# Shift and scale of the first layer: VectorE sums five of eight row blocks, and one unread product is left out

## The chip, the cores and the metric

The kernel runs on one core of one Trainium2 chip, as one program. The metric is the device time of one execution in microseconds (us).

## What is computed

Two blocks of two layers each, on 512 positions of width 1024, in 32-bit floats. The part that matters here is the start of the first layer: from a vector `c` six vectors of width 1024 are made, and the first two, shift and scale, enter the normalized input ahead of the layer's first product.

```python
c_act = jax.nn.silu(c)
mod = c_act @ w_ada + b_ada                     # 1024 -> 6 * 1024
shift1, scale1, gate1, shift2, scale2, gate2 = jnp.split(mod, 6, axis=-1)
h = modulate(rms_norm(x, norm1_g), shift1, scale1)     # h * (1 + scale1) + shift1
... = jnp.split(h @ w_in, split_points, axis=-1)
```

Everything behind that (retention, gated linear attention, forgetting attention, the feed-forward parts, and the second block with its pooling and windowed attention) is the same in both kernels.

## The kernel before, in words

All activations lie transposed: `x[k]` holds 128 of the 1024 features (k = 0 to 7) by 512 positions. Weights stream through the kernel as 486 chunks `w` of eight 128x128 tiles. A product in full precision is made from three matmuls in a faster 32-bit format (`mm3`, lines 219 to 221): every operand is split in a high and a low part, `wh` and `wl` for weights, `h[k][:, 0]` and `h[k][:, 1]` for activations, and the products high by high, high by low and low by high are added in PSUM. For each chunk ScalarE casts `wh` (line 184) and VectorE subtracts for `wl` (line 193); `prep_to(c)` issues both for all chunks up to c.

The schedule is manual: each engine executes its instructions in the order in which the Python code issues them, and waits at each for what that instruction needs.

The opening is `start_group` (line 1094). It computes the first seven output tiles of `h @ w_in` (`nj` = 7), and makes shift, scale and `h` block by block as it goes:

- `ada_dma(k)` loads, for block k, the 256 columns of `w_ada` (128 of shift and 128 of scale) in two tiles of 128x(4x256): the row blocks kk = 0 to 3 and 4 to 7 of the 1024 rows.
- `ada_pe(k)` (line 1128) multiplies the eight row blocks with `cpad[:, kk]`, a 128x32 tile whose column 0 is `c_act` and whose other columns are zero. Each such matmul fills 32 columns of TensorE's array, and four lie side by side (`tile_position=(0, c)`); row blocks 4 to 7 are a second round on the same four places. The result is one row of 256 in each of four groups of 32 PSUM partitions. ScalarE copies it to `row` (line 1134).
- `ada_ab(k)` (line 1138) adds the four groups and turns the row into two columns, with two matmuls against a column of ones (line 1141); VectorE adds the bias (line 1143) and forms (1 + scale) times the norm's gain (line 1144). The two columns of `AB` are what this text calls AB of block k.
- `norm_s(k)`: VectorE makes `nt` = x times AB's scale times the reciprocal norm (line 324), ScalarE adds the shift and rounds to the high half of `h[k]` (line 329), VectorE subtracts for the low half (line 336).

Ahead of the loop stand the sum of squares, its sum over the partitions (`colsum`, line 296), the reciprocal root on GpSimd (line 301), and `bcast` (line 306), which spreads the reciprocal norm over the partitions. In between, `busy(k)` (line 1158) issues a product of `ident` and `x[k]` into a PSUM buffer that nobody reads.

The loop over k is the place of the change. One step multiplies block k with its seven tiles. After the tiles j = 0, 1 and 4 the work for later blocks is woven in (`early`):

```python
if i == 0:      norm_s(k + 1, pB)
elif i == 1:    ada_pe(k + 2); prep_to(...)
elif i == 2:    ada_ab(k + 2)
```

In step 0 the order is a different one: the seven tiles are passed three times, and `ada_pe(1)`, `ada_pe(2)` and their `ada_ab` stand between the passes.

PSUM holds five buffers `mm` and three `sd`. Seven of the eight carry the seven sums of the loop; the last `sd` serves `ada_pe` and `ada_ab` of one block after the other.

Of the kernel before, what the change touches and what calls it, by code (L numbers as in the profile page):

```python
# [10 lines left out]
F32 = mybir.dt.float32  # L11
F32R = mybir.dt.float32r
AF = mybir.ActivationFunctionType
ALU = mybir.AluOpType
# [93 lines left out]
def emit(tc, A, log, stop=None, dump=None):  # L108
    nc = tc.nc
    ctx = ExitStack()  # L110
    sb = ctx.enter_context(tc.tile_pool(name="sb", bufs=1))
# [4 lines left out]
    def nm(p):  # L116
        uid[0] += 1
        return f"{p}_{uid[0]}"

    def g4(p, dt=F32, shape=(128, 1024)):  # L120
        return sb.tile(list(shape), dt, tag="g4", bufs=NG, name=nm(p))

    def t2(p, dt=F32):
        return sb.tile([128, 512], dt, tag="t2", bufs=NT, name=nm(p))

    def c16(p, dt=F32):
        return sb.tile([128, 16], dt, tag="c16", bufs=20, name=nm(p))

    def mmb():
        return pp.tile([128, 512], F32, tag="mm", bufs=5, name=nm("mm"))  # L130

    def sdb():
        return pp.tile([128, 512], F32, tag="sd", bufs=3, name=nm("sd"))

    V, ACT, PL, PE = nc.vector, nc.scalar, nc.gpsimd, nc.tensor
# [24 lines left out]
    def pc(key, l=None, i=0, n=1):  # L160
        o = _PO[key if l is None else (key, l)] + i
        return par[:, o:o + n]
# [9 lines left out]
    def w_dma(c):  # L172
        while st["dma"] <= min(c, NCH - 1):
            t = g4("w")
            nc.sync.dma_start(t, wall[st["dma"]])
            stage[st["dma"]] = t
            st["dma"] += 1

    def w_hi(c):
        while st["hi"] <= min(c, NCH - 1):  # L180
            i = st["hi"]
            w_dma(i)
            his[i] = g4("wh", F32R)
            ACT.copy(his[i], stage[i])  # L184
            st["hi"] += 1

    def prep_to(c, eng=None):
        while st["prep"] <= min(c, NCH - 1):
            i = st["prep"]
            w_dma(i + 1 + LD)  # L190
            w_hi(i + st["ha"])
            l = g4("wl", F32R)
            (eng or V).tensor_tensor(l, stage.pop(i), his[i].bitcast(F32), op=ALU.subtract)  # L193
            prepped[i] = (his.pop(i), l)
            st["prep"] += 1
# [96 lines left out]
    def colsum(out, sq, c0, n):  # L292

        p = sdb()
        for i in range(n):
            PE.transpose(p[:, i * 128:(i + 1) * 128], sq[:, c0 + i * 128:c0 + (i + 1) * 128], ident)  # L296
        V.tensor_reduce(out, p[:, 0:n * 128].rearrange("p (a b) -> p a b", a=n), axis=AX.X, op=ALU.add)

    def rstd_of(r, n, dim):
        V.tensor_scalar(r, r, 1.0 / dim, EPS, op0=ALU.mult, op1=ALU.add)  # L300
        PL.tensor_tensor(r, r, mhalf[:, 0:n], op=ALU.pow)

    def bcast(ps, r, n):

        for i in range(n):
            PE.transpose(ps[:, i * 128:(i + 1) * 128], r[:, i:i + 1].to_broadcast([128, 128]), ident)
# [11 lines left out]
    def new_h():  # L318
        for k in range(8):
            h[k] = sb.tile([128, 2, 512], F32R, tag="h", bufs=8, name=nm("h"))  # L320
# [216 lines left out]
    cact = sb.tile([128, 8], F32, name="cact")  # L537
# [556 lines left out]
    def start_group(cons):  # L1094
        specs, evacs, view = cons
        nj = len(evacs)
        st["la"] = st["ha"] = 0
        cpad = sb.tile([128, 8, 32], F32, name="cpad")
        PL.memset(cpad, 0.0)
        ACT.activation(cact, pc("c", None, 0, 8), AF.Silu)  # L1100
        V.tensor_copy(cpad[:, :, 0], cact)
        at = {}

        def ada_dma(k):
            at[k] = []
            for j in range(2):
                t = g4("ada", shape=(128, 4, 256))
                nc.sync.dma_start(t, A["wada"][2 * k + j].rearrange("p (a b) -> p a b", a=4))
                at[k].append(t)

        for k in range(8):
            nc.sync.dma_start(x[k], A["xT"][k * 128:(k + 1) * 128])
        ada_dma(0)
        w_dma(0)
        ada_dma(1)
        w_dma(1)
        ada_dma(2)
        w_dma(2)
        ada_dma(3)
        ada_dma(4)  # L1120
        AB = c16("AB")
        bpair = c16("bp")
        V.tensor_copy(bpair.rearrange("p (k j) -> p j k", j=2), pc("bada", 0, 0, 16).rearrange("p (j k) -> p j k", j=2))
        Ac, Bc = (lambda k: AB[:, 2 * k + 1:2 * k + 2]), (lambda k: AB[:, 2 * k:2 * k + 1])
        pa, ra = {}, {}

        def ada_pe(k):

            pa[k] = p = sdb()
            for kk in range(8):  # L1130
                c = 32 * (kk % 4)
                PE.matmul(p[c:c + 32, 0:256], cpad[:, kk], at[k][kk // 4][:, kk % 4], start=kk < 4, stop=kk >= 4, tile_position=(0, c))
            ra[k] = t2("row")[:, 0:256]
            ACT.copy(ra[k], p[:, 0:256])
            del at[k]

        def ada_ab(k):

            p, row = pa.pop(k), ra.pop(k)
            for i in range(2):  # L1140
                PE.matmul(p[:, 256 + i:257 + i], row[:, i * 128:(i + 1) * 128], one, start=True, stop=True)
            ab = AB[:, 2 * k:2 * k + 2]
            V.tensor_tensor(ab, p[:, 256:258], bpair[:, 2 * k:2 * k + 2], op=ALU.add)
            V.tensor_scalar(ab[:, 1:2], ab[:, 1:2], 1.0, pc("n1", 0, k), op0=ALU.add, op1=ALU.mult)

        acc = sb.tile([128, 512], F32, tag="acc", bufs=1, name=nm("acc"))
        for k in range(8):
            if k == 0:
                ACT.activation(acc, x[k], AF.Square)
            else:  # L1150
                q = t2("sq")
                ACT.activation(q, x[k], AF.Square)
                V.tensor_tensor(acc, acc, q, op=ALU.add)
        spare = mmb()

        def busy(k):

            PE.matmul(spare, ident, x[k], start=True, stop=True)

        for k in range(5):  # L1160
            busy(k)
        r = c16("rs")
        colsum(r[:, 0:4], acc, 0, 4)
        rstd_of(r[:, 0:4], 4, D)
        ada_pe(0)
        ada_ab(0)
        busy(5)
        pb = sdb()
        bcast(pb, r, 4)
        busy(6)  # L1170
        new_h()
        w_hi(0)

        def norm_s(k, pB):
            t = norm_t(k, 0, 512, pB, Ac)
            norm_h(k, 0, 512, t, Bc)
            norm_l(k, 0, 512, t, Bc)

        t = norm_t(0, 0, 512, pb, Ac)
        norm_h(0, 0, 512, t, Bc)  # L1180
        prep_to(0)
        norm_l(0, 0, 512, t, Bc)
        pB = t2("rB")
        ACT.copy(pB, pb)
        ps = [mmb() for _ in range(5)] + [sdb() for _ in range(nj - 5)]
        for k in range(8):
            if 4 < k + 4 < 8:
                ada_dma(k + 4)
            if k == 4:
                nc.sync.dma_start(cst, A["cst"])  # L1190
                st.pop("late", lambda: None)()
            ts = [take(specs(k, j)) for j in range(nj)]
            xh, xl = h[k][:, 0], h[k][:, 1]

            def early(i):

                if i == 0:
                    norm_s(k + 1, pB)
                    if k == 0:
                        prep_to(1)  # L1200
                elif i == 1 and k < 6:
                    ada_pe(k + 2)
                    prep_to(((k + 2) * nj + nj - 1) // 8)
                elif i == 2 and k < 6:
                    ada_ab(k + 2)

            if k == 0:
                for j in range(nj):
                    PE.matmul(ps[j], tw(ts[j])[0], xh, start=True, stop=False)
                ada_pe(1)  # L1210
                for j in range(nj):
                    PE.matmul(ps[j], tw(ts[j])[0], xl, start=False, stop=False)
                ada_ab(1)
                early(0)
                for j in range(nj):
                    PE.matmul(ps[j], tw(ts[j])[1], xh, start=False, stop=False)
                    if j == 2:
                        early(1)
                early(2)
            else:  # L1220
                for j in range(nj):
                    mm3(ps[j], ts[j], (xh, xl), False, k == 7)
                    if j in (0, 1, 4) and k < 7:
                        early((0, 1, 4).index(j))
            if k >= 5:
                prep_to((k + 1) * nj // 8 + k - 5)
        st["la"], st["ha"] = LA, 1
        for j in range(nj):
            evacs[j](ps[j])
        adaq.append(ada_gen())  # L1230
# [554 lines left out]
```

## Time and profile before

| what | us |
|---|---|
| three runs, median | 2881.34 |
| three runs, lowest to highest | 2876.54 to 2883.03 |
| the profiled execution, its own time | 2873.25 |
| the profiled execution, span of the trace | 2871.5 |
| TensorE (PE) busy with matmuls in the span | 2846.4 |
| VectorE (DVE) busy | 1457.7 |
| ScalarE (ACT) busy | 983.5 |
| GpSimd (POOL) busy | 416.8 |

The profile is of one execution. Its span runs from the first to the last instruction; its own time is 1.75 us longer than the span. A share of busy time is an average over all stages of the kernel; what one edit is worth is read from the stage that it touches. PE are matmuls, PEld loads of weights into the array, which lie beside them. The record of a matmul is longer than the distance to the next one, as matmuls are pipelined; the distance between starts is the pace. A full 32-bit matmul leaves two records.

### The profile page before, as it was taken

How to read it: one execution, taken by the hardware profiler on the slowest of the kernel's cores; microseconds unless marked ns; L12 is line 12 of the kernel's file. 1: busy time of each engine (PE TensorE's matmuls, PEld its weight loads, DVE VectorE, ACT ScalarE, POOL GpSimd, SP SyncE). 2: the span in 40 equal slices, each digit the busy share in tenths (PEclk: the TensorE clock that was granted, in tenths of full speed). 3: DMA queues.
4: the chain of work that ended last, by engine and by line, in shares of the span. 5: the costliest groups of instructions: out<-in, count | busy, mean ns of one | idle time of the engine just before them, and what ended most of it. 6: DMA issues, size and time to landing. Idle time of an engine off the chain costs nothing.

```text
span 2871.5 us, 34084 instructions
## 1 busy us (share of the span) xinstructions
PE 2846.4 (99%) x13840; PEld 2371.8 (83%) x13840; DVE 1457.7 (51%) x1972; ACT 983.5 (34%) x1462; POOL 416.8 (15%) x286
## 2 busy tenths in 40 slices
PE   9999999999999999999999999999999999999998
PEld 6888878888888888878888888788888888888887
DVE  5868575675444545454454343763333565553333
ACT  4143333333233234333343133342222354432122
POOL 0212020110011221120111011221011211110011
PEclk9999999999999999999999999999999999999999
DMA  8445434444323222223322323232332322322321
GB/s 316 149 145 191 154 105 151 144 151 154 118 90 117 88 83 94 88 74 94 105 96 90 116 81 96 79 120 81 100 106 88 103 80 86 110 85 96 103 88 52
DMA packets 92513, 320.56 MB, mean 112 GB/s; under 512 B 10011, under 2 KB 14269, under 8 KB 92357
## 3 DMA queue, kind: packets, MB, share of 16 engines
q1 hardware_dynamic: 87620, 312.87, 33.1%
q10 hardware_dynamic: 4736, 5.52, 0.6%
q8 instruction: 108, 1.77, 0.3%
q14 instruction: 49, 0.39, 0.0%
HBM read 314.93 MB, written 3.42 MB: 111 GB/s over the span
## 4 chain that ended last, share of the span: by engine, by line
PE 95%; DVE 2%; ACT 1%; DMA 1%; issue 0%; POOL 0%; ACTq 0%; SPq 0%; DVEq 0%; POOLq 0%
PE mm L219 26%; PE mm L221 26%; PE mm L220 26%; PE mm L282 3%; PE mm L284 3%; PE mm L283 3%; PE sd L679 1%; PE sd L953 1%; PE sd L296 0%; PE sd L220 0%; PE sd L219 0%; PE sd L221 0%; PE sd L1450 0%; DVE wl L193 0%; DMA scr<-vs 0%
## 5 line engine op out<-in xcount | busy, mean ns | idle before, releaser
L219 PE MATMUL mm<-h,wh 128*128 128x512 f32 (+1 forms) x2323 | 893.6, 385 | 0.0
L221 PE MATMUL mm<-h,wl 128*128 128x512 f32 (+1 forms) x2323 | 887.0, 382 | 0.3 <-DVE wl L193 0.3
L220 PE MATMUL mm<-h,wh 128*128 128x512 f32 (+1 forms) x2323 | 887.3, 382 | 0.0
L193 DVE TENSOR_TENSOR wl<-w,wh 128x1024 fp32r<-128x1024 f32 x486 | 631.5, 1306 | 62.1 <-ACT wh L184 57.2
L184 ACT CAST wh<-w 128x1024 fp32r<-128x1024 f32 x486 | 500.1, 1046 | 187.6 <-DVE wl L193 77.0
L219 PEld LDWEIGHTS mm<-h,wh 128*128 128x128 f32 x2323 | 437.2, 188 | 86.2 <-issue 3.1
L221 PEld LDWEIGHTS mm<-h,wl 128*128 128x128 f32 x2323 | 437.1, 188 | 86.2 <-DVE wl L193 0.8
L220 PEld LDWEIGHTS mm<-h,wh 128*128 128x128 f32 x2323 | 437.4, 188 | 82.6
L219 PE MATMUL mm<-y,wh 128*128 128x512 f32 (+1 forms) x704 | 269.3, 383 | 0.0
L220 PE MATMUL mm<-y,wh 128*128 128x512 f32 (+1 forms) x704 | 269.2, 382 | 0.0
L221 PE MATMUL mm<-y,wl 128*128 128x512 f32 (+1 forms) x704 | 269.2, 382 | 0.0
L282 PE MATMUL mm<-wh,h 128*128 128x512 f32 (+1 forms) x448 | 170.8, 381 | 0.0
L284 PE MATMUL mm<-wl,h 128*128 128x512 f32 (+1 forms) x448 | 168.1, 375 | 0.0
L283 PE MATMUL mm<-wh,h 128*128 128x512 f32 (+1 forms) x448 | 168.1, 375 | 0.0
L1030 DVE TENSOR_TENSOR g<-g,mm 128x512 f32<-128x512 f32 x44 | 30.3, 688 | 264.5 <-PE mm L221 263.4
L220 PEld LDWEIGHTS mm<-y,wh 128*128 128x128 f32 x704 | 132.3, 188 | 25.9
L221 PEld LDWEIGHTS mm<-y,wl 128*128 128x128 f32 x704 | 132.3, 188 | 25.8
L219 PEld LDWEIGHTS mm<-y,wh 128*128 128x128 f32 x704 | 132.3, 188 | 25.6
L310 POOL TENSOR_TENSOR y<-u,y 128x512 fp32r<-128x512 f32 x44 | 68.2, 1551 | 525.2 <-ACT y L309 515.9
L310 POOL TENSOR_TENSOR y<-g,y 128x512 fp32r<-128x512 f32 x44 | 67.9, 1543 | 520.9 <-ACT y L309 520.9
L384 POOL TENSOR_TENSOR acc<-acc,sq 128x512 f32<-128x512 f32 x48 | 69.1, 1440 | 481.7 <-ACT sq L383 481.1
L572 DVE SCALAR_TENSOR_TENSOR adaacc<-ada,cact,adaacc 128x512 f32<-128x512 f32 x140 | 127.6, 911 | 3.0
(369 smaller groups left out, 3150.3 us busy)
## 6 DMA issues: line engine op xcount, KB each, us to landing
w<-in_wall SPq DMA_DIRECT2D x486, 512.0 KB, 3.5
ada<-in_wada SPq DMA_DIRECT2D x96, 512.0 KB, 3.5
x<-in_xT SPq DMA_DIRECT2D x8, 256.0 KB, 5.3
cB<-scr ACTq DMA_DIRECT2D x8, 256.0 KB, 4.6
cR<-in_cr SPq DMA_DIRECT2D x2, 512.0 KB
cD<-in_cd SPq DMA_DIRECT2D x2, 512.0 KB, 7.3
c<-in_cd SPq DMA_DIRECT2D x2, 512.0 KB
scr<-vs ACTq DMA_DIRECT2D x4, 256.0 KB, 4.7
```

The costliest lines, as they stand in the source:

```text
L184: ACT.copy(his[i], stage[i])
L193: (eng or V).tensor_tensor(l, stage.pop(i), his[i].bitcast(F32), op=ALU.subtract)
L219: PE.matmul(ps, wh, xh, start=start, stop=False)
L220: PE.matmul(ps, wh, xl, start=False, stop=False)
L221: PE.matmul(ps, wl, xh, start=False, stop=stop)
L282: PE.matmul(ps[tb][:, 0:ncol], xh, wh, start=k == 0, stop=False)
L283: PE.matmul(ps[tb][:, 0:ncol], xl, wh, start=False, stop=False)
L284: PE.matmul(ps[tb][:, 0:ncol], xh, wl, start=False, stop=k == 7)
L310: (eng or V).tensor_tensor(hl[:, 1], src, hl[:, 0].bitcast(F32), op=ALU.subtract)
L384: PL.tensor_tensor(sqa["acc"], sqa["acc"], q, op=ALU.add)
L572: V.scalar_tensor_tensor(acc, src, cact[:, kk:kk + 1], acc, op0=ALU.mult, op1=ALU.add)
L1030: V.tensor_tensor(s, s, ps, op=ALU.mult)
```

## The change

It adds `ada_sum(k)`: VectorE forms, from the loaded tiles, the sum over row blocks kk = 3 to 7 of `w_ada` times the per-partition scalar `c_act[:, kk]`, a 128x256 tile `as` that is not yet summed over its partitions. One TENSOR_SCALAR starts it, four SCALAR_TENSOR_TENSOR add to it. `ada_pe(k)` then has one round of four matmuls: row blocks 0, 1 and 2 with `cpad`, and `as` with `opad`, a tile whose column 0 is ones. `ada_sum(k + 2)` is issued in steps 1 to 5 behind `norm_s(k + 1)`, so blocks 3 to 7 have one round and blocks 0 to 2 still two. In the steps from 1 on, `ada_pe` and `prep_to` move from behind tile j = 1 to behind j = 4, and `ada_ab` from behind j = 4 to behind j = 6, the step's last tile. Of the seven products that nobody reads six are left, and the sixth stands behind `bcast` now.

```diff
@@ -1099,6 +1099,9 @@
         PL.memset(cpad, 0.0)
         ACT.activation(cact, pc("c", None, 0, 8), AF.Silu)
         V.tensor_copy(cpad[:, :, 0], cact)
+        opad = sb.tile([128, 32], F32, name="opad")
+        PL.memset(opad, 0.0)
+        PL.memset(opad[:, 0:1], 1.0)
         at = {}
 
         def ada_dma(k):
@@ -1122,14 +1125,27 @@
         bpair = c16("bp")
         V.tensor_copy(bpair.rearrange("p (k j) -> p j k", j=2), pc("bada", 0, 0, 16).rearrange("p (j k) -> p j k", j=2))
         Ac, Bc = (lambda k: AB[:, 2 * k + 1:2 * k + 2]), (lambda k: AB[:, 2 * k:2 * k + 1])
-        pa, ra = {}, {}
+        pa, ra, asum = {}, {}, {}
+
+        def ada_sum(k):
+
+            asum[k] = a = t2("as")[:, 0:256]
+            V.tensor_scalar(a, at[k][0][:, 3], cact[:, 3:4], None, op0=ALU.mult)
+            for kk in range(4, 8):
+                V.scalar_tensor_tensor(a, at[k][1][:, kk - 4], cact[:, kk:kk + 1], a, op0=ALU.mult, op1=ALU.add)
 
         def ada_pe(k):
 
             pa[k] = p = sdb()
-            for kk in range(8):
-                c = 32 * (kk % 4)
-                PE.matmul(p[c:c + 32, 0:256], cpad[:, kk], at[k][kk // 4][:, kk % 4], start=kk < 4, stop=kk >= 4, tile_position=(0, c))
+            if k in asum:
+                for kk in range(4):
+                    c = 32 * kk
+                    w, r = (cpad[:, kk], at[k][0][:, kk]) if kk < 3 else (opad, asum.pop(k))
+                    PE.matmul(p[c:c + 32, 0:256], w, r, start=True, stop=True, tile_position=(0, c))
+            else:
+                for kk in range(8):
+                    c = 32 * (kk % 4)
+                    PE.matmul(p[c:c + 32, 0:256], cpad[:, kk], at[k][kk // 4][:, kk % 4], start=kk < 4, stop=kk >= 4, tile_position=(0, c))
             ra[k] = t2("row")[:, 0:256]
             ACT.copy(ra[k], p[:, 0:256])
             del at[k]
@@ -1164,10 +1180,9 @@
         rstd_of(r[:, 0:4], 4, D)
         ada_pe(0)
         ada_ab(0)
-        busy(5)
         pb = sdb()
         bcast(pb, r, 4)
-        busy(6)
+        busy(5)
         new_h()
         w_hi(0)
 
@@ -1198,6 +1213,8 @@
                     norm_s(k + 1, pB)
                     if k == 0:
                         prep_to(1)
+                    elif k < 6:
+                        ada_sum(k + 2)
                 elif i == 1 and k < 6:
                     ada_pe(k + 2)
                     prep_to(((k + 2) * nj + nj - 1) // 8)
@@ -1220,8 +1237,8 @@
             else:
                 for j in range(nj):
                     mm3(ps[j], ts[j], (xh, xl), False, k == 7)
-                    if j in (0, 1, 4) and k < 7:
-                        early((0, 1, 4).index(j))
+                    if j in (0, 4, 6) and k < 7:
+                        early((0, 4, 6).index(j))
             if k >= 5:
                 prep_to((k + 1) * nj // 8 + k - 5)
         st["la"], st["ha"] = LA, 1
```

How the order of the instructions moves, at three places. In these rows the names are those of the program with a number of their own (`as_300` is the sum of block 3), and `x3` counts equal instructions. Line numbers of the changed kernel are 3 to 17 higher in this part.

VectorE in steps 1 and 2, before (`AB_132`, `nt_294`, `h_197` belong to block 2; `AB_132`, `nt_344`, `h_198` further down to block 3):

```order
L1143 TENSOR_TENSOR AB_132<-sd_262,bp_133 128x2 [waits PE_49]
L1144 TENSOR_SCALAR AB_132<-AB_132,par 128x1 [waits DVE_49]
L324 SCALAR_TENSOR_TENSOR nt_294<-x_68,AB_132,rB_211 128x512 [waits DVE_49]
L336 SCALAR_TENSOR_TENSOR h_197<-nt_294,AB_132,h_197 128x512 [waits Activation_49]
L193 TENSOR_TENSOR wl_316<-w_253,wh_314 128x1024 [waits DMAHW6_49,Activation_49]
L1143 TENSOR_TENSOR AB_132<-sd_301,bp_133 128x2 [waits PE_49]
L1144 TENSOR_SCALAR AB_132<-AB_132,par 128x1 [waits DVE_49]
L324 SCALAR_TENSOR_TENSOR nt_344<-x_69,AB_132,rB_211 128x512 [waits DMAHW4_49,DVE_49]
L336 SCALAR_TENSOR_TENSOR h_198<-nt_344,AB_132,h_198 128x512 [waits Activation_49]
```

and with the change (`as_300` and the second AB are of block 3):

```order
L1159 TENSOR_TENSOR AB_135<-sd_264,bp_136 128x2 [waits PE_49]
L1160 TENSOR_SCALAR AB_135<-AB_135,par 128x1 [waits DVE_49]
L324 SCALAR_TENSOR_TENSOR nt_296<-x_68,AB_135,rB_213 128x512 [waits DVE_49]
L336 SCALAR_TENSOR_TENSOR h_199<-nt_296,AB_135,h_199 128x512 [waits Activation_49]
L1133 TENSOR_SCALAR as_300<-ada_127,cact 128x256 [waits DMAHW2_49]
L1135 SCALAR_TENSOR_TENSOR as_300<-ada_129,cact,as_300 128x256 [waits DMAHW3_49,DVE_49]
L1135 SCALAR_TENSOR_TENSOR as_300<-ada_129,cact,as_300 128x256 [waits DVE_49] x3
L193 TENSOR_TENSOR wl_329<-w_255,wh_327 128x1024 [waits DMAHW6_49,Activation_49]
L1159 TENSOR_TENSOR AB_135<-sd_318,bp_136 128x2 [waits PE_49]
L1160 TENSOR_SCALAR AB_135<-AB_135,par 128x1 [waits DVE_49]
L324 SCALAR_TENSOR_TENSOR nt_348<-x_69,AB_135,rB_213 128x512 [waits DMAHW4_49,DVE_49]
```

The five instructions of the sum now stand between the low half of `h` and `wl`, and AB of the next block still stands behind `wl`.

TensorE in step 1, before, from the end of the tile j = 1 on (`ada_124` and `ada_126` are block 3's two loaded tiles):

```order
L221 MATMUL mm_214<-h_196,wl_257 128x512 [waits DVE_49]
L1132 MATMUL sd_301<-ada_124,cpad 32x256 [waits DMAHW2_49,DVE_49]
L1132 MATMUL sd_301<-ada_124,cpad 32x256 x3
L1132 MATMUL sd_301<-ada_126,cpad 32x256 [waits DMAHW3_49]
L1132 MATMUL sd_301<-ada_126,cpad 32x256 x3
L219 MATMUL mm_215<-h_196,wh_255 128x512
L220 MATMUL mm_215<-h_196,wh_255 128x512
L221 MATMUL mm_215<-h_196,wl_257 128x512
```

and with the change, from the end of the tile j = 4 on:

```order
L221 MATMUL mm_219<-h_198,wl_259 128x512
L1144 MATMUL sd_318<-ada_127,cpad 32x256 [waits DMAHW2_49,DVE_49]
L1144 MATMUL sd_318<-ada_127,cpad 32x256 x2
L1144 MATMUL sd_318<-as_300,opad 32x256 [waits DVE_49]
L219 MATMUL sd_220<-h_198,wh_257 128x512
L220 MATMUL sd_220<-h_198,wh_257 128x512
L221 MATMUL sd_220<-h_198,wl_259 128x512
L219 MATMUL sd_221<-h_198,wh_257 128x512
L220 MATMUL sd_221<-h_198,wh_257 128x512
L221 MATMUL sd_221<-h_198,wl_259 128x512
L1157 MATMUL sd_318<-ones,row_323 128x1 [waits Activation_49]
L1157 MATMUL sd_318<-ones,row_323 128x1
```

The eight matmuls of block 3 have become four, the fourth waits for VectorE's sum, the group stands three tiles later, and L1141 (now L1157) is behind the last tile.

TensorE at the start, between the first `ada_ab` and the first tile, before (`sd_189<-ident,rs_164` is `bcast`):

```order
L1141 MATMUL sd_173<-ones,row_182 128x1 [waits Activation_49]
L1141 MATMUL sd_173<-ones,row_182 128x1
L1158 MATMUL mm_158<-x_71,ident 128x512 [waits DMAHW6_49]
L306 MATMUL sd_189<-ident,rs_164 128x128 [waits Pool_49]
L306 MATMUL sd_189<-ident,rs_164 128x128 x3
L1158 MATMUL mm_158<-x_72,ident 128x512 [waits DMAHW7_49]
L1209 MATMUL mm_213<-h_195,wh_203 128x512 [waits Activation_49]
```

and with the change:

```order
L1157 MATMUL sd_176<-ones,row_185 128x1 [waits Activation_49]
L1157 MATMUL sd_176<-ones,row_185 128x1
L306 MATMUL sd_191<-ident,rs_167 128x128 [waits Pool_49]
L306 MATMUL sd_191<-ident,rs_167 128x128 x3
L1174 MATMUL mm_161<-x_71,ident 128x512 [waits DMAHW6_49]
L1226 MATMUL mm_215<-h_197,wh_205 128x512 [waits Activation_49]
```

`bcast` now directly follows the first `ada_ab`, and one product with `ident` is left behind it.

## Rows read from the trace of the kernel before

**Rows 1.** The page's part 1: busy time, share of the span, instructions, by engine.

```profile
PE 2846.4 (99%) x13840; PEld 2371.8 (83%) x13840; DVE 1457.7 (51%) x1972; ACT 983.5 (34%) x1462; POOL 416.8 (15%) x286
```

**Rows 2.** The page's part 4: the chain that ended last, by engine.

```profile
PE 95%; DVE 2%; ACT 1%; DMA 1%; issue 0%; POOL 0%; ACTq 0%; SPq 0%; DVEq 0%; POOLq 0%
```

**Rows 3.** Timeline, start of the opening: start us, us, engine, line, operation, out<-in, count [idle].

```profile
14.00 1.02 POOL L301 TENSOR_TENSOR rs<-rs,mhalf 128x4 f32<-128x4 f32 x1 [12.48 <-DVE rs L300]
14.47 0.61 PE L1141 MATMUL sd<-ones,row 128*128 128x1 f32 x4 [0.49 <-ACT row L1134]
14.94 1.10 PE L1158 MATMUL mm<-x,ident 128*128 128x512 f32 x2
15.88 0.60 PE L306 MATMUL sd<-ident,rs 128*128 128x128 f32 x4
16.52 0.75 DVE L324 SCALAR_TENSOR_TENSOR nt<-x,AB,sd 128x512 f32<-128x512 f32 x1 [0.93 <-PE sd L306]
```

**Rows 4.** Timeline of TensorE, steps 3 to 5 of the opening.

```profile
44.93 0.50 PE L1141 MATMUL sd<-ones,row 128*128 128x1 f32 x4
...
46.76 0.40 PE L219 MATMUL mm<-h,wh 128*128 128x512 f32 x1
...
48.24 1.07 PE L1132 MATMUL sd<-ada,cpad 128*32 128x256 f32 x16
49.24 0.50 PE L219 MATMUL mm<-h,wh 128*128 128x512 f32 x1
...
51.44 0.50 PE L1141 MATMUL sd<-ones,row 128*128 128x1 f32 x4
...
57.95 0.50 PE L1141 MATMUL sd<-ones,row 128*128 128x1 f32 x4
```

**Rows 5.** Timeline of VectorE, steps 1, 3 and 4 of the opening.

```profile
30.50 0.75 DVE L336 SCALAR_TENSOR_TENSOR h<-nt,AB,h 128x512 fp32r<-128x512 f32 x1 [0.79 <-ACT h L329]
...
45.47 0.16 DVE L1143 TENSOR_TENSOR AB<-sd,bp 128x2 f32<-128x2 f32 x1
...
47.46 0.75 DVE L336 SCALAR_TENSOR_TENSOR h<-nt,AB,h 128x512 fp32r<-128x512 f32 x1 [0.79 <-ACT h L329]
50.78 1.23 DVE L193 TENSOR_TENSOR wl<-w,wh 128x1024 fp32r<-128x1024 f32 x1 [2.57 <-ACT wh L184]
51.98 0.16 DVE L1143 TENSOR_TENSOR AB<-sd,bp 128x2 f32<-128x2 f32 x1
```

**Rows 6.** Timeline of ScalarE, step 4 of the opening.

```profile
49.43 0.37 ACT L1134 COPY row<-sd 128x256 f32<-128x256 f32 x1 [2.00 <-PE sd L1132]
49.70 1.05 ACT L184 CAST wh<-w 128x1024 fp32r<-128x1024 f32 x1
```

**Rows 7.** Timeline of TensorE, one visit: its first and its second round.

```profile
35.22 0.42 PE L1132 MATMUL sd<-ada,cpad 128*32 128x256 f32 x4
35.68 0.61 PE L1132 MATMUL sd<-ada,cpad 128*32 128x256 f32 x8
```

**Rows 8.** Groups by line and shape, count | busy, mean ns; then a chained pair's timeline.

```profile
L324 DVE SCALAR_TENSOR_TENSOR nt<-x,ab,sd 128x256 f32<-128x256 f32 x48 | 22.3, 475 | 7.4 <-PE sd L306 7.4
L967 DVE TENSOR_SCALAR fe<-fe,fs 128x256 f32<-128x256 f32 x8 | 2.8, 344 | 0.0
599.31 1.53 DVE L572 SCALAR_TENSOR_TENSOR adaacc<-ada,cact,adaacc 128x512 f32<-128x512 f32 x2
```

**Rows 9.** Stretches of 1 us (busy us per engine, PEclk, DMA), and matmuls from TensorE's timeline.

```profile
1859.00:1860.00 1.00, 0.38 (x1) 0.19 (x1) 0.40 (x1) 1.00 (x2) 0.00 (x0) 1.00 0.53 213
...
1861.00:1862.00 1.00, 1.00 (x4) 0.81 (x3) 1.00 (x2) 0.00 (x0) 0.00 (x0) 0.50 0.49 82
...
2444.00:2445.00 1.00, 0.00 (x0) 0.00 (x0) 1.00 (x5) 0.16 (x1) 0.00 (x0) 1.00 0.46 45
...
1861.69 0.63 PE L220 MATMUL sd<-p,wh 128*128 128x512 f32 x1
1862.12 0.63 PE L221 MATMUL sd<-p,wl 128*128 128x512 f32 x1
```

## The prediction

> **What bounds the kernel now.** I read the page first: matrix products fill 99% of the span, VectorE about half [rows 1], and 95% of the chain that ended last lies on TensorE [rows 2]. So a microsecond that TensorE waits is a microsecond of the result, and work on VectorE costs nothing as long as TensorE doesn't wait for it. Outside the first 60 us nothing is edited, so the rest of the reading is a timeline of the opening, engine by engine.
>
> Call step k the 21 matmuls that use row block k of x, and a visit the matmuls of one `ada_pe`. On TensorE the steps repeat every 6.51 us: `ada_ab`'s matmuls (L1141) start at 44.93 and again at 51.44 [rows 4]. TensorE has no wait for data in there; the visit of 48.24 to 49.24 runs through. On VectorE one step is: `wl`, the two small AB instructions, `nt`, a gap while ScalarE makes the high half of `h`, the low half of `h`, then nothing until ScalarE has cast the next `wh` [rows 5]. The point to see is the order: `wl` stands ahead of AB, because ScalarE casts `wh` only behind the copy of `row` [rows 6]. Before, this is harmless, as a visit needs only loaded weights and a PSUM buffer: no arrow runs from VectorE's `nt` and `h` to the next visit.
>
> **The change, part by part.**
>
> *The opening product.* `bcast` (L306) stood behind a product that nobody reads. It began at 15.88; its input was ready at 14.00 + 1.02 = 15.02 and the matmuls ahead of that product ended at 14.47 + 0.61 = 15.08 [rows 3]. So it can start at 15.10: **0.78 us earlier**, and `nt` of block 0 with it (15.74 for 16.52). The product that is left is now behind `bcast`, in the time in which TensorE waits for `h` anyway. The two added memsets on GpSimd fall into its idle time ahead of 14.00.
>
> *One round instead of two.* A visit's second round starts 0.46 us behind the first (35.22 and 35.68, [rows 7]), so a visit with one round is 0.46 us shorter; the time around it (switching into and out of the narrow tiles) stays. The order shows that five visits change, those of blocks 3 to 7: a gain of at most 5 x 0.46 = **2.3 us**, and a step of 6.51 - 0.46 = 6.05 us if TensorE never waits.
>
> *The sum on VectorE.* Per block one TENSOR_SCALAR and four chained SCALAR_TENSOR_TENSOR of 128x256. Instructions of these kinds and widths took 344 ns and 475 ns; a chained pair of twice the width took 1.53 us for two of 0.75, so some 0.03 us lies between links [rows 8]. The sum is 0.34 + 4 x 0.475 + 4 x 0.04 = 2.40 us, 2.44 with the start. The bounds are close: 2.24 us without any gap, 2.60 with gaps of twice the length. Its inputs have landed: TensorE reads the same tiles earlier in the old kernel than VectorE does in the new one.
>
> *Where the sum stands.* In VectorE's queue it is behind the low half of `h` and ahead of `wl`; on TensorE the round that needs it is behind five of the step's seven tiles. This closes a loop of one step: AB of block k lets `nt` go, then `h` high, `h` low, then the sum of block k+1, the last matmul of that block's round, `row`, the cast of `wh`, `wl`, and only behind `wl` AB of block k+1. Each link from the rows:
> - AB to the end of the low half: 45.47 to 47.46 + 0.75 = 48.21, 2.74 us [rows 5]; the sum 2.44. Together 5.18.
> - From the end of the sum: 0.04 to start the matmul, 0.73 to `row` (visit at 48.24, `row` at 49.43, less the one round of 0.46; [rows 4, 6]), 0.27 to the cast (49.43 to 49.70), 1.08 to `wl` (49.70 to 50.78), 1.20 to AB (50.78 to 51.98) [rows 5, 6]. Together 3.32.
>
> The loop takes 5.18 + 3.32 = **8.50 us a step**, against 6.51 before and the 6.05 that TensorE needs. TensorE thus stands still for some 2.4 us in each visit, in front of the one matmul that reads the sum.
>
> *The sum over the opening.* The low half of block 2 ended at 30.50 + 0.75 = 31.25 [rows 5]; with the 0.78 gained, at 30.47. The sum for block 3 is ready at 32.91, and with four loops of 8.50 the one for block 7 at 66.91. TensorE then takes 0.04, the rest of the visit (1.00 - 0.46 = 0.54), six matmuls (1.47, at the pace of the nine from 49.24 to 51.44) and L1141 (1.83 from 44.93 to 46.76, less six matmuls: 0.36), and step 6 starts at 69.32. Before it started at 57.95 + 1.83 = 59.78 [rows 4]. The step starts **9.5 us late**. Nothing behind it gives this back: from there on TensorE is the bound, and the later loads only get more time.
>
> *The clock* is taken as full in this sum. The bound from below is 1.00, which the opening shows now; the bound from above is a fall to 0.50, which the trace shows twice, near 1860 after a stretch in which TensorE was busy 38% of a microsecond, while a full stop of about 1.5 us near 2444 left it at 1.00 [rows 9]. I take 1.00, as the steps here are dense around one wait. The Trainium skill, TensorE: Matmul & The Clock Gate, section "HAM oscillation — how this bites in real kernels", says that matmuls issued in short bursts with waits between them find the clock halved again after each wait. By that rule the time would be that of the second rival below; near 1860 this trace agrees with it (0.50), near 2444 it does not.
>
> The profiled execution took 2873.25 us, 8 us under the median of the three runs, so it would become 2882.8. Against the median, 2881.34 + 9.5 = **2890.8 us**.
>
> **The rivals.**
> 1. *VectorE has room, and TensorE finds the sum ready.* For it: VectorE idles for 0.79 + 2.57 = 3.36 us in a step of 6.51 [rows 5], so it works some 3.1, and 2.4 more is 5.5, under 6.05. It decides if the sum is ready before TensorE has finished five tiles, some 3.8 us after the step's start; that needs the sum to run in the gap that `wl` waits in, without holding up anything behind it. Then the change gives 0.78 + 2.3 = 3.1 us: 2878.2, not slower. Against it: the order has `nt`, `h`, the sum, `wl` and AB in one queue, and the gap ahead of `wl` exists only because `row` comes late, which now waits for the sum itself.
> 2. *The loop, and the clock falls in its waits.* At half clock a 512-column matmul follows the last one after 0.43 us (1861.69 to 1862.12) [rows 9] in place of the 2.20 / 9 = 0.24 of the opening [rows 4]. The six matmuls and L1141 behind the sum then end at about 0.04 + 1.0 + 6 x 0.43 + 0.7 = 4.3 us in place of the 3.32 of the `wl` path, and become the longer way: 1.0 us more a loop, at most 4 us over four: up to 2895. For it: no wait inside the opening's steps is as long now as the 2.4 us to come.
> 3. *Part of the loop overlaps.* If the cast of `wh` and `wl` were not in the loop, AB would wait for L1141 alone: 0.04 + 0.54 + 1.47 + 0.36 = 2.4 instead of 3.32, a loop of 7.6 us, and some 6 us of loss: 2887. Against it stands the order of ScalarE and VectorE, in which nothing can pass.
>
> **How the numbers follow.** Two versions of this kernel can be told apart from about 0.2%, 5.8 us. Forecast 0.62, rival 2 0.22, rival 1 0.08, rival 3 0.08. The forecast's own range is 2887 to 2894 (the bounds of VectorE's sum, some 0.2 us either way, five times, and the spread of the runs, 2876.54 to 2883.03). Downward the range goes to 2884, which takes in rival 3; upward rival 2 with its 2895 and the spread of the runs set 2897. Rival 1 is left out below. Slower by over 0.2%: nearly all of the forecast and rival 2 and half of rival 3, less what the spread can hide, 0.82. Within 0.2%: rival 1, which is a gain of 0.1%, and the rest, 0.15. Faster by over 0.2%: only rival 1 with a lucky spread, 0.03.
>
> **What would show it.** In the changed profile: the visits of blocks 3 to 7 should start about 8.5 us apart, each with a wait of over 2 us that ends with VectorE's sum; `nt` of block 0 near 15.7; the five sum instructions together near 2.4 us; AB directly behind `wl`; step 6 starting near 69 us in place of 59.8; everything behind shifted by the same amount. The prediction is wrong if the visits stay 6 us apart with no wait on the sum, if the sum's instructions take far less than 0.48 us each, or if a later stage gives the loss back. A granted clock of 0.5 between 33 and 70 us would show rival 2.

## The result, and the profile after

| | before | after |
|---|---|---|
| runs of this comparison, median, us | 2878.94 (2872.51 to 2883.03, 4 runs) | 2927.1 (2924.16 to 2930.59, 4 runs) |
| ratio, 95% interval | | 1.0169 [1.0155, 1.0184] |
| the profiled execution, us | 2873.25 | 2926.18 |
| its span, us | 2871.5 | 2924.4 |

The change makes the kernel 48.2 us slower. The forecast was 2890.8, with a range of 2884 to 2897: right in its sign, and five times too small. The time lies 30 us above the range's upper end.

The first look goes to the opening, where all the edits are. Part 1 of the page of the changed kernel, and the first line of part 4 (the chain that ended last, by engine):

```profile
PE 2893.1 (99%) x13798; PEld 2377.6 (81%) x13798; DVE 1467.1 (50%) x1997; ACT 983.8 (34%) x1462; POOL 417.9 (14%) x288
PE 95%; DVE 3%; ACT 1%; issue 1%; POOL 0%; DMA 0%; ACTq 0%; SPq 0%; DVEq 0%; POOLq 0%
```

VectorE is hardly busier (1467.1 for 1457.7) and the chain's share on it went from 2% to 3%. But TensorE's busy time rose by 46.7 us [rows 1], although it has 42 records fewer. A wait alone can't do that: TensorE is *busy* longer.

TensorE in the opening of the changed kernel, as the timeline shows it (start us, us, engine, line, operation, out<-in, count, idle before and its releaser). L1144 is `ada_pe`'s matmul, now in two pieces: the round's first three matmuls, then the one that reads the sum `as`.

```profile
29.58 0.63 PE L1144 MATMUL sd<-ada,cpad 128*32 128x256 f32 x6
32.66 0.62 PE L1144 MATMUL sd<-as,opad 128*32 128x256 f32 x2 [2.44 <-DVE as L1135]
...
41.66 0.62 PE L1144 MATMUL sd<-as,opad 128*32 128x256 f32 x2 [0.71 <-DVE as L1135]
...
50.00 0.62 PE L1144 MATMUL sd<-as,opad 128*32 128x256 f32 x2 [1.63 <-DVE as L1135]
...
58.28 0.62 PE L1144 MATMUL sd<-as,opad 128*32 128x256 f32 x2 [1.59 <-DVE as L1135]
...
66.57 0.62 PE L1144 MATMUL sd<-as,opad 128*32 128x256 f32 x2 [1.59 <-DVE as L1135]
...
70.07 0.77 PE L219 MATMUL mm<-h,wh 128*128 128x512 f32 x1
```

The waits in front of the sum are there, in all five visits, and VectorE's sum ends each; 2.44 us is the first, the others are 0.71 to 1.63. From one to the next it takes 9.00, 8.34, 8.28 and 8.29 us. Step 6 starts at 70.07 where it started at 59.78 [rows 4]: 10.3 us late. VectorE and ScalarE around the first of these loops:

```profile
30.18 0.34 DVE L1133 TENSOR_SCALAR as<-ada,cact 128x256 f32<-128x256 f32 x1
30.55 2.04 DVE L1135 SCALAR_TENSOR_TENSOR as<-ada,cact,as 128x256 f32<-128x256 f32 x4
34.72 1.23 DVE L193 TENSOR_TENSOR wl<-w,wh 128x1024 fp32r<-128x1024 f32 x1 [2.12 <-ACT wh L184]
36.51 0.16 DVE L1159 TENSOR_TENSOR AB<-sd,bp 128x2 f32<-128x2 f32 x1 [0.57 <-PE sd L1157]
```

```profile
33.37 0.37 ACT L1150 COPY row<-sd 128x256 f32<-128x256 f32 x1 [3.90 <-PE sd L1144]
33.63 1.05 ACT L184 CAST wh<-w 128x1024 fp32r<-128x1024 f32 x1
```

The sum takes from 30.18 to 30.55 + 2.04 = 32.59, that is 2.41 us. The matmul follows at 32.66, `row` at 33.37, the cast at 33.63, `wl` at 34.72: the links run one behind the other. AB should stand directly behind `wl`, near 35.9; it comes at 36.51, after 0.57 us idle that ends with TensorE (L1157 is `ada_ab`'s matmul, L1141 before). The reason is the granted clock, the number behind the busy times in these stretches (busy us of PE, PEld, DVE, ACT, POOL, then PEclk, DMA share, GB/s):

```profile
34.00:36.00 2.00, 2.00 (x8) 1.61 (x6) 1.23 (x1) 0.68 (x1) 0.00 (x0) 0.50 1.02 408
...
48.00:50.00 2.00, 0.37 (x7) 0.01 (x1) 1.83 (x4) 0.00 (x0) 0.00 (x0) 1.00 0.19 73
50.00:52.00 2.00, 2.00 (x8) 1.37 (x9) 0.00 (x0) 1.32 (x2) 0.00 (x0) 1.00 0.00 0
...
68.00:70.00 2.00, 2.00 (x8) 1.62 (x6) 0.00 (x0) 0.00 (x0) 0.00 (x0) 0.50 0.60 240
```

It is 0.50 (1.2 GHz) behind the first wait and behind the last one, and 1.00 (2.4 GHz) behind a wait in between, with TensorE busy 0.37 of 2 us ahead of it.

So the opening loses 10.3 us. The span grew by 2924.4 - 2871.5 = 52.9. **42.6 us are lost behind step 6, where no edit is.** Part 5 of the page says where, in its groups of matmuls that read `h` (count | busy us, mean ns of one):

```profile
L219 PE MATMUL mm<-h,wh 128*128 128x512 f32 (+1 forms) x2323 | 904.0, 389 | 0.0
L221 PE MATMUL mm<-h,wl 128*128 128x512 f32 (+1 forms) x2323 | 898.1, 387 | 0.1
L219 PE MATMUL mm<-y,wh 128*128 128x512 f32 (+1 forms) x704 | 269.4, 383 | 0.0
L282 PE MATMUL mm<-wh,h 128*128 128x512 f32 (+1 forms) x448 | 172.6, 385 | 0.0
```

The same groups on the page of before, with the same counts:

```profile
L219 PE MATMUL mm<-h,wh 128*128 128x512 f32 (+1 forms) x2323 | 893.6, 385 | 0.0
L221 PE MATMUL mm<-h,wl 128*128 128x512 f32 (+1 forms) x2323 | 887.0, 382 | 0.3 <-DVE wl L193 0.3
L219 PE MATMUL mm<-y,wh 128*128 128x512 f32 (+1 forms) x704 | 269.3, 383 | 0.0
L282 PE MATMUL mm<-wh,h 128*128 128x512 f32 (+1 forms) x448 | 170.8, 381 | 0.0
```

Each group with `h` in it costs 4 to 5 ns more per matmul, whether `h` is streamed (L219 to L221) or held in the array as the weight (L282 to L284); L220, L283 and L284 read alike. The group that streams `y` costs 0.1 us more in 269. A record is longer than the distance to the next matmul, so the loss itself is read from the pace. The first and the last of 24 matmuls on `h` that follow each other without a gap, before and then after (not the same 24: at this time the changed kernel is some 18 us late already):

```profile
500.14 0.39 PE L219 MATMUL mm<-h,wh 128*128 128x512 f32 x1
...
505.36 0.39 PE L221 MATMUL mm<-h,wl 128*128 128x512 f32 x1
```

```profile
501.44 0.40 PE L219 MATMUL mm<-h,wh 128*128 128x512 f32 x1
...
506.80 0.39 PE L221 MATMUL mm<-h,wl 128*128 128x512 f32 x1
```

5.22 us for 23 distances before, 5.36 after: 227.0 and 233.0 ns. Over all unbroken runs of ten or more in eight stretches of the trace the pace is 227.3 ns before and 232.4 after where `h` is streamed, 226.7 and 232.9 where it is held, and on `y` it stays near 227. Priced out: 3 x 2323 = 6969 matmuls by 5.1 ns and 3 x 448 = 1344 by 6.2 ns are 43.9 us, against the 42.6 to be explained.

What can change the pace of a matmul that nobody edited? Not the granted clock: its mean is 0.992 to 0.997 over the four executions of the changed kernel and 0.993 to 0.998 over those of before. But `opad` is a new tile of 128 bytes in each partition, and it is allocated ahead of `h`. In the compiled programs `h` begins at byte 185,824 of a partition before and at 185,952 after. The weight buffers, a ring that begins at byte 38,112 with a pitch of 4096 bytes, lie where they lay, and so do `y` and `br`, which take their buffers from that ring. Before, `h` thus begins 577 x 256 bytes behind the ring; with the change, 128 bytes more.

### The profile page after: what moved, and what is told of

It reads as the page before. It is cut to its first block, busy times and chain, and to the rows that moved or that the text cites. A ratio compares the mean times of both kernels' runs of the same rounds, so it can differ in the third digit from the quotient of the medians.

```text
span 2924.4 us, 34027 instructions
## 1 busy us (share of the span) xinstructions
PE 2893.1 (99%) x13798; PEld 2377.6 (81%) x13798; DVE 1467.1 (50%) x1997; ACT 983.8 (34%) x1462; POOL 417.9 (14%) x288
## 4 chain that ended last, share of the span: by engine, by line
PE 95%; DVE 3%; ACT 1%; issue 1%; POOL 0%; DMA 0%; ACTq 0%; SPq 0%; DVEq 0%; POOLq 0%
PE mm L219 26%; PE mm L221 26%; PE mm L220 26%; PE mm L284 3%; PE mm L283 3%; PE mm L282 3%; PE sd L679 1%; PE sd L953 1%; DVE wl L193 0%; PE sd L296 0%; PE sd L220 0%; PE sd L221 0%; PE sd L219 0%; PE sd L1467 0%; DVE as L1135 0%
## 5 line engine op out<-in xcount | busy, mean ns | idle before, releaser
L219 PE MATMUL mm<-h,wh 128*128 128x512 f32 (+1 forms) x2323 | 904.0, 389 | 0.0
L221 PE MATMUL mm<-h,wl 128*128 128x512 f32 (+1 forms) x2323 | 898.1, 387 | 0.1
L220 PE MATMUL mm<-h,wh 128*128 128x512 f32 (+1 forms) x2323 | 897.9, 387 | 0.0
L221 PEld LDWEIGHTS mm<-h,wl 128*128 128x128 f32 x2323 | 437.1, 188 | 96.8 <-DVE wl L193 0.6
L219 PEld LDWEIGHTS mm<-h,wh 128*128 128x128 f32 x2323 | 437.4, 188 | 94.9 <-issue 1.0
L220 PEld LDWEIGHTS mm<-h,wh 128*128 128x128 f32 x2323 | 437.5, 188 | 93.7
L219 PE MATMUL mm<-y,wh 128*128 128x512 f32 (+1 forms) x704 | 269.4, 383 | 0.0
L221 PE MATMUL mm<-y,wl 128*128 128x512 f32 (+1 forms) x704 | 269.3, 383 | 0.0
L220 PE MATMUL mm<-y,wh 128*128 128x512 f32 (+1 forms) x704 | 269.3, 382 | 0.0
L282 PE MATMUL mm<-wh,h 128*128 128x512 f32 (+1 forms) x448 | 172.6, 385 | 0.0
L284 PE MATMUL mm<-wl,h 128*128 128x512 f32 (+1 forms) x448 | 170.2, 380 | 0.0
L283 PE MATMUL mm<-wh,h 128*128 128x512 f32 (+1 forms) x448 | 170.0, 380 | 0.0
L221 PEld LDWEIGHTS mm<-y,wl 128*128 128x128 f32 x704 | 132.3, 188 | 25.9
L219 PEld LDWEIGHTS mm<-y,wh 128*128 128x128 f32 x704 | 132.3, 188 | 25.9
L220 PEld LDWEIGHTS mm<-y,wh 128*128 128x128 f32 x704 | 132.3, 188 | 25.8
```

Source lines behind the costliest of these rows:

```text
L219: PE.matmul(ps, wh, xh, start=start, stop=False)
L220: PE.matmul(ps, wh, xl, start=False, stop=False)
L221: PE.matmul(ps, wl, xh, start=False, stop=stop)
L282: PE.matmul(ps[tb][:, 0:ncol], xh, wh, start=k == 0, stop=False)
L283: PE.matmul(ps[tb][:, 0:ncol], xl, wh, start=False, stop=False)
L284: PE.matmul(ps[tb][:, 0:ncol], xh, wl, start=False, stop=k == 7)
```

## The experiments

The theory: **placement**. `h` lies 128 bytes further from the weights than before, and that distance sets the pace of a matmul that reads both; the sum and its waits cost the opening's 9 to 10 us and nothing else. The rival: **order**. The opening, now in another order, leaves loads, buffers or the clock in another state, and the rest of the kernel runs slower behind it. Times are medians in us with the lowest and highest run; the ratio is to runs of before on the same chip.

**1. The change, with `opad` allocated behind `h`.** Nothing else differs from the changed kernel.

```diff
-        opad = sb.tile([128, 32], F32, name="opad")
-        PL.memset(opad, 0.0)
-        PL.memset(opad[:, 0:1], 1.0)
         at = {}
...
         new_h()
+        opad = sb.tile([128, 32], F32, name="opad")
+        PL.memset(opad, 0.0)
+        PL.memset(opad[:, 0:1], 1.0)
         w_hi(0)
```

> The changed kernel, with the tile of ones (opad) allocated behind the tiles h instead of ahead of them, so that every tile up to h lies where it lay before; the instructions are the same. Placement theory: the opening still starts step 6 some 10 us late, but matmuls on h follow each other after 0.227 us again instead of 0.232, and the time is about 2879 + 10 = 2889 us. Order theory (the new order of loads and weight buffers costs the rest all along the kernel): 2927 us as in the changed kernel, matmuls on h still at 0.232.

2887.16 (2886.93 to 2888.99), before 2878.48; ratio 1.0032 [1.0018, 1.0045]. The pace on `h` is 227.2 streamed and 226.8 held. Its page's groups, and the waits on the sum in its timeline (L1141 and L1132 are L1144 and L1135 of the changed kernel):

```profile
L219 PE MATMUL mm<-h,wh 128*128 128x512 f32 (+1 forms) x2323 | 893.9, 385 | 0.0
L282 PE MATMUL mm<-wh,h 128*128 128x512 f32 (+1 forms) x448 | 170.8, 381 | 0.0
```

```profile
32.83 0.59 PE L1141 MATMUL sd<-as,opad 128*32 128x256 f32 x2 [2.56 <-DVE as L1132]
...
41.15 0.62 PE L1141 MATMUL sd<-as,opad 128*32 128x256 f32 x2 [1.67 <-DVE as L1132]
...
49.96 0.62 PE L1141 MATMUL sd<-as,opad 128*32 128x256 f32 x2 [0.58 <-DVE as L1132]
...
58.24 0.62 PE L1141 MATMUL sd<-as,opad 128*32 128x256 f32 x2 [1.66 <-DVE as L1132]
...
67.08 0.62 PE L1141 MATMUL sd<-as,opad 128*32 128x256 f32 x2 [0.59 <-DVE as L1132]
...
69.49 0.49 PE L219 MATMUL mm<-h,wh 128*128 128x512 f32 x1
```

The five waits are all still there and the pace is back. This is the price of the order alone: 8.7 us, with step 6 at 69.49, against 9.5 and 69.32 in the prediction. 39.5 of the 48.2 us go away with the place of one small tile.

**2. The kernel before, with an unused tile of 128 bytes where `opad` stands.**

```diff
         PL.memset(cpad, 0.0)
+        gap = sb.tile([128, 32], F32, name="gap")
+        PL.memset(gap, 0.0)
```

> The kernel before, with an unused tile of 128 bytes per partition allocated where the change allocates opad, and nothing else. Placement theory: the opening as before (step 6 near 59.8), matmuls on h at 0.232 us, 2879 + 37 = about 2916 us. Order theory: 2879 us, no change.

2921.05 (2915.5 to 2926.56), before 2878.48; ratio 1.0150 [1.0129, 1.0171]. Pace 232.4 streamed, 233.0 held, 227.2 on `y`.

```profile
L219 PE MATMUL mm<-h,wh 128*128 128x512 f32 (+1 forms) x2323 | 903.5, 389 | 0.0
L282 PE MATMUL mm<-wh,h 128*128 128x512 f32 (+1 forms) x448 | 172.6, 385 | 0.0
```

Nothing of the change is in this kernel but 128 bytes that nobody reads, and it loses 42.6 us. The opening's loss and this one together are 8.7 + 42.6 = 51.3 for the 48.2 of the whole change. With experiment 1 the order theory falls.

**3. The same, with 256 bytes** (`[128, 64]`).

> The kernel before with an unused tile of 256 bytes per partition at that place. If what counts is the place of h within 256 bytes, h is back where it was and the time is 2879 us; if any other place than that of before is slow, about 2916 us; order theory: 2879 us.

2881.39 (2876.23 to 2884.01 in nine runs, 7421.47 in the tenth, which the ratio leaves out and for which nothing on record gives a cause), before 2878.48; ratio 1.0008 [0.9998, 1.0018]; pace 227.4 and 226.7. So it isn't that a tile was added, or that `h` moved: by 256 bytes it costs nothing.

**4. 128 bytes ahead of everything, so that weights and `h` both move.**

```diff
     nc.vector.memset(mhalf, -0.5)
+    gap = sb.tile([128, 32], F32, name="gap")
+    nc.gpsimd.memset(gap, 0.0)
```

> The kernel before with 128 unused bytes per partition ahead of the weight buffers as well as of h, so that both move together. If the distance of h to the weights counts, matmuls on h stay at 0.227 us and the time at 2879 us. If the place of the operand itself counts, those on h slow down to 0.232 us, and those on y, which lies in the weights' buffers, too: 2916 + 2112 x 0.0056 = about 2928 us. Order theory: 2879 us.

2880.49 (2870.65 to 2882.72), before 2878.48; ratio 1.0005 [0.9993, 1.0017]; pace 227.3 and 226.7. `h` lies at the address that was slow in experiment 2, and is fast. What counts is where it lies to the weights, not where it lies. One thing stays untested: the small tiles allocated between `cpad` and `h` moved with `h` in every run, so no run moves `h` alone. That matmuls on `y` keep their pace beside them (227.2 in experiment 2) speaks for `h`.

**5. Experiment 1, with the sum made a step earlier and ahead of the low half of `h`.** This undoes the queue loop and keeps the single round. The visits are back behind the tiles 0, 1 and 4.

```diff
-        def norm_s(k, pB):
+        def norm_s(k, pB, between=None):
             t = norm_t(k, 0, 512, pB, Ac)
             norm_h(k, 0, 512, t, Bc)
+            if between is not None:
+                ada_sum(between)
             norm_l(k, 0, 512, t, Bc)
...
-                    norm_s(k + 1, pB)
+                    norm_s(k + 1, pB, k + 3 if 0 < k < 5 else None)
                     if k == 0:
                         prep_to(1)
-                    elif k < 6:
-                        ada_sum(k + 2)
...
-                    if j in (0, 4, 6) and k < 7:
-                        early((0, 4, 6).index(j))
+                    if j in (0, 1, 4) and k < 7:
+                        early((0, 1, 4).index(j))
```

> As the run with the tile of ones behind h, but the sum of block k + 3 is made in step k between nt and the low half of h (blocks 4 to 7; block 3 has two rounds again), and visits and ada_ab stand after the tiles 0, 1 and 4 as before. Loop theory: no matmul waits for a sum of its own step, so TensorE runs through; step 6 starts near 57.2 in place of 59.8, and the time is 2878.5 - 0.8 - 4 x 0.46 = about 2876 us. If VectorE's extra 2.4 us a step are themselves too much, visits still wait and step 6 starts after 60.

2877.57 (2873.98 to 2880.58, 11 runs), before 2878.81; ratio 0.9993 [0.9984, 1.0002]. TensorE's timeline, `ada_ab`'s matmuls (L1154 here), then one step of VectorE:

```profile
14.82 0.61 PE L1154 MATMUL sd<-ones,row 128*128 128x1 f32 x4 [0.49 <-ACT row L1147]
...
49.70 0.50 PE L1154 MATMUL sd<-ones,row 128*128 128x1 f32 x4
...
55.77 0.50 PE L1154 MATMUL sd<-ones,row 128*128 128x1 f32 x4
```

```profile
45.28 0.35 DVE L1130 TENSOR_SCALAR as<-ada,cact 128x256 f32<-128x256 f32 x1
45.66 2.05 DVE L1132 SCALAR_TENSOR_TENSOR as<-ada,cact,as 128x256 f32<-128x256 f32 x4
47.63 0.75 DVE L336 SCALAR_TENSOR_TENSOR h<-nt,AB,h 128x512 fp32r<-128x512 f32 x1
```

No wait on the sum is left. The steps are 6.07 us apart, from 6.51 [rows 4]. From the first `ada_ab` to the last it takes 40.95 us, and 57.95 - 14.47 = 43.48 before [rows 3, 4]: 2.53 us gained in the trace. The runs give 1.2 us with an interval from 4.6 gained to 0.6 lost, so by the times alone it can't be told from before. It is 49.5 us ahead of the change. Several things differ from experiment 1 at once (the sum is made a step earlier and ahead of the low half, and the visits stand elsewhere); which of them is needed was not tested.

**6. Only the unread product taken out of the kernel before** (one run).

```diff
-        busy(5)
         pb = sdb()
         bcast(pb, r, 4)
-        busy(6)
+        busy(5)
```

> The kernel before with the one unread product less and bcast directly behind the first ada_ab, nothing else. Both theories: nt of block 0 near 15.7, step 6 near 59.0 in place of 59.8, the whole 0.8 us shorter, which the times alone cannot show.

The one run took 2882.27, inside the range of before beside it (2873.82 to 2883.99); for 0.8 us only the trace can speak.

```profile
14.84 0.61 PE L1141 MATMUL sd<-ones,row 128*128 128x1 f32 x4 [0.49 <-ACT row L1134]
...
57.54 0.50 PE L1141 MATMUL sd<-ones,row 128*128 128x1 f32 x4
```

```profile
16.13 0.75 DVE L324 SCALAR_TENSOR_TENSOR nt<-x,AB,sd 128x512 f32<-128x512 f32 x1 [0.17 <-PE sd L306]
```

From the first `ada_ab` matmul to `nt` it is 16.13 - 14.84 = 1.29 us, and 16.52 - 14.47 = 2.05 before [rows 3]. From the first to the last `ada_ab` it is 42.70 for 43.48. They give 0.76 and 0.78 us: all of it reaches the end of the opening.

**7. to 12. Experiment 2 with other sizes of the unused tile.** The diff is that of experiment 2 with N = 16, 8, 48, 24, 40 and 56 floats in `[128, N]`, that is 64, 32, 192, 96, 160 and 224 bytes.

> The kernel before with 64 unused bytes ahead of h. If the slowdown depends on the distance of h to the weights within 256 bytes in a smooth way, matmuls on h lie between 0.227 and 0.232 us and the time between 2879 and 2921; if it is there or not there by the distance alone, it is either of the two ends. Order theory: 2879.

> The kernel before with 32 unused bytes ahead of h. Same question as with 64 bytes: 2879 if distances under 128 bytes are as good as none, 2921 if any distance costs, a time below 2879 if the place of before is not the best one.

> The kernel before with 192 unused bytes ahead of h. With 64 bytes, matmuls that stream h followed each other after 229.2 ns and those that hold h as weights after 233.3 ns. If the distance of the streamed operand to the held one counts, with its sign and within 256 bytes, 192 is the mirror of 64: streaming h 233 ns, holding h 229 ns, and the time 2879 + about 40 = 2919 us. If only the size of the distance counts, both are as with 64 bytes, 2897 us.

> 96 unused bytes. If 0 (and 64 in part) are exceptions and every other distance costs the full price, 233 ns and about 2921 us; if some distance is better than 0, below 226.7 ns and below 2879 us.

> 160 unused bytes. Same question as with 96: 233 ns and about 2921 us if it is no exception, less than 226.7 ns if the place of before is not the best. Order theory, for all of these: 2879 us.

> 224 unused bytes, the mirror of 32: 233 ns both ways and about 2922 us.

| unused bytes | median, us | ratio, interval | pace, `h` streamed, ns | `h` held, ns |
|---|---|---|---|---|
| 0 (before) | 2878.48 to 2881.26 | 1 | 227.3 | 226.7 |
| 32 | 2922.57 | 1.0152 [1.0139, 1.0166] | 233.3 | 233.3 |
| 64 | 2896.58 | 1.0065 [1.0051, 1.0079] | 229.2 | 233.3 |
| 96 | 2923.67 | 1.0151 [1.0127, 1.0175] | 233.4 | 234.1 |
| 128 | 2921.05 | 1.0150 [1.0129, 1.0171] | 232.4 | 233.0 |
| 160 | 2931.41 | 1.0177 [1.0152, 1.0201] | 234.2 | 233.3 |
| 192 | 2919.41 | 1.0137 [1.0113, 1.0160] | 233.3 | 231.7 (229.6 in the whole trace) |
| 224 | 2925.24 | 1.0150 [1.0119, 1.0180] | 233.3 | 233.3 |
| 256 | 2881.39 | 1.0008 [0.9998, 1.0018] | 227.4 | 226.7 |

The row at 64 stands out on the page as well: the group that holds `h` is as slow as at 128 bytes (173.0 and 172.6 us), the one that streams it lies between before and 128 bytes (900.1, between 893.6 and 903.5). By the pace the streamed one has about a third of the loss, 1.9 of 6 ns.

```profile
L219 PE MATMUL mm<-h,wh 128*128 128x512 f32 (+1 forms) x2323 | 900.1, 387 | 0.0
L282 PE MATMUL mm<-wh,h 128*128 128x512 f32 (+1 forms) x448 | 173.0, 386 | 0.0
```

If the two operands only changed places, 192, which is 64 short of 256, would be the mirror of 64: held at 229, streamed at 233. By the eight stretches it came out at 231.7 and 233.3, but 231.7 is a mixture. In the whole trace 28 of 30 unbroken runs with `h` held go at 228.7 to 229.5 ns, and two at 233.3; the longer of the two supplies 95 of the 150 distances in the eight stretches. The first and the 25th matmul, in that run and then in one of the 28:

```profile
1000.39 0.40 PE L282 MATMUL mm<-wh,h 128*128 128x512 f32 x1
...
1005.99 0.40 PE L282 MATMUL mm<-wh,h 128*128 128x512 f32 x1
```

```profile
1186.59 0.39 PE L282 MATMUL mm<-wh,h 128*128 128x512 f32 x1
...
1192.09 0.39 PE L282 MATMUL mm<-wh,h 128*128 128x512 f32 x1
```

The 24 distances take 5.60 us (233.3 ns) and 5.50 (229.2). The two at 233.3 are the only ones of the 30 that follow without a break behind matmuls that stream `h`, which go at 233.3 there; why they keep that pace isn't known. So the mirror holds, these two apart, and it holds in the other rows too: 96 streamed and 160 held read 233.4 and 233.3, 160 streamed and 96 held 234.2 and 234.1. What counts is the distance from the held operand to the streamed one, with its sign and modulo 256. The time expected for 192 by that rule was 2919 us; measured are 2919.41.

Of the eight places in steps of 32 bytes the one that the kernel before has is the best, and no other comes near it.

## Why the prediction was right in the opening and wrong in all

- **"So it can start at 15.10: 0.78 us earlier"**: right. Experiment 6 shows 0.76 to 0.78.
- **"A visit with one round is 0.46 us shorter", "a step of 6.05 us if TensorE never waits"**: right. Experiment 5 shows steps of 6.07 (0.44 shorter).
- **"The sum is 0.34 + 4 x 0.475 + 4 x 0.04 = 2.40 us"**: right, 2.41.
- **"The loop takes 8.50 us a step"**: right to some 0.2 us. With the clock full it took 8.28 to 8.34, and all five waits end with VectorE's sum. Its sign "each with a wait of over 2 us" held for the first alone: a visit at the full clock is 2.24 us longer than in experiment 5 (47.74 to 50.55, against 46.95 to 47.52), but only 1.63 of that is recorded as idle. The first sum was ready at 32.59 for 32.91, the last was read at 66.57 for 66.95. Rival 1 (room on VectorE) and rival 3 (part of the loop overlaps) didn't happen here; experiment 5 shows that rival 1 is right in the size of VectorE's room and only needs another order, with the sum made a step earlier.
- **"I take 1.00"** for the clock: wrong at two of five waits. Rival 2 had the mechanism and nearly the price: behind the first wait AB waited 0.57 us for `ada_ab`'s slowed matmul and the loop took 9.00, 0.7 more than the others; behind the last, 3.50 us passed to step 6 in place of 0.54 + 1.47 + 0.36 = 2.37. The 1.13 us there, less the 0.38 by which the last sum was read early, are the difference of 70.07 to 69.32. In experiment 1, with the same instructions, the clock fell elsewhere (behind the second and the fourth wait, not behind the first, which was the longest at 2.56 us; rows below). So the length of the wait alone doesn't decide it. The prediction's "which the trace shows twice" misses a third fall: behind those near 1860 and 2376 the trace of before has one at its end (0.50 from 2864 on). The Trainium skill, TensorE: Matmul & The Clock Gate, section "HAM oscillation — how this bites in real kernels", which the prediction weighed, has the clock halved again after each wait, in a kernel whose waits are longer than any here: here it fell after two of five. The stretches of experiment 1 behind the first, the second and the fourth wait, in the columns of those above:

```profile
34.00:36.00 2.00, 2.00 (x12) 1.70 (x11) 1.13 (x1) 0.84 (x1) 0.00 (x0) 1.00 1.02 406
...
42.00:44.00 2.00, 2.00 (x7) 1.55 (x6) 0.79 (x1) 1.18 (x2) 0.00 (x0) 0.57 1.02 401
...
60.00:62.00 2.00, 2.00 (x8) 1.72 (x8) 1.29 (x2) 0.21 (x1) 0.00 (x0) 0.50 0.71 283
```

- **The step that failed: "Outside the first 60 us nothing is edited, so the rest of the reading is a timeline of the opening"**, and with it "Nothing behind it gives this back", where the only question asked of the rest was whether it would give the loss back. Experiments 1 and 2 show what stands in its place: the new tile moves `h` by 128 bytes against the weights, and the 8313 matmuls that read `h`, nearly all of them behind the opening, take 5 to 6 ns longer each, 42.6 us. The two memsets of `opad` were costed (they fall into GpSimd's idle time); its place in memory was not. The prediction's sum of 9.5 us is the price of what it looked at: experiment 1 has 8.7.

No row of the trace before holds this price, since `h` has one place in it. What could have been seen is that an allocation stands ahead of others, that 8313 matmuls read one of the tiles behind it, and that 1% of their pace is 19 us.

Open is why the distance matters: the runs show that it does, that its sign counts and what each place costs, not the mechanism. The Trainium skill, SBUF — State Buffer, section "Who interferes with whom", gives TensorE two independent read ports and says that it never waits on anyone. Whoever reads from it that the operands' places are free would expect experiment 2 to cost nothing; it cost 1.5%, and the measurement decides.

## What to carry to other kernels

A new buffer is an edit to every instruction that reads a buffer allocated behind it: allocate it last, or pad it so that what lies behind moves by a multiple of 256 bytes (256 itself is the one that was tried, and it was free), and compare the pace of long runs of matmuls, operand by operand, before looking for a reason in the schedule. When TensorE's *busy* time rises by 1.6% with the same matmuls and the same granted clock, no wait explains it. And before work moves to an engine with idle time, follow its queue once around: VectorE had 3.4 us free in a step, and the sum cost 2 us a step where the same step's matmuls waited for it, and nothing where it was made a step earlier.

## What the runs showed of the hardware

The pace of a 512-column matmul, each with its own load of weights, depends on the distance in memory from the held operand to the streamed one. At the distance of before, a multiple of 256 bytes, and at 256 bytes more it is 226.7 to 227.4 ns; at 64 bytes more it is 229.2 ns; at the other six steps of 32 bytes it is 232.4 to 234.2 (the table above). The sign counts: where `h` moves by 64 bytes it goes at 229.2 streamed and 233.3 held, and where it moves by 192 it goes at 233.3 streamed and, in 28 of 30 unbroken runs, at 228.7 to 229.5 held. In a kernel in which TensorE is busy 99% of the span this is 0.65 to 1.8% of the time.
